# Sums of the last weights: in DRAM by copying and adding transfers during the SwiGLU pairs, in place of GpSimd sums inside the last product

## The chip, the cores and the metric

The kernel runs on one core of one Trainium2 chip. TensorE (PE) multiplies, PEld is its weight load, VectorE is DVE, ScalarE is ACT, GpSimd is POOL, and SyncE (SP) issues most DMA transfers. The metric is the device time of one execution in microseconds (us). The kernel before takes 820.69 us, the median of 3 runs (820.62 to 823.06).

## The reference, cut to what matters

One decoder block on 512 tokens of width 1024 in float32: a norm, one wide product `h @ w_in`, a causal convolution mixer and a recurrent mixer side by side, their merge through `w_mix_out`, then the SwiGLU channel mixer and a last norm. The change concerns the channel mixer:

```python
    h = rmsnorm(x, norm2_g[l])
    x = x + (jax.nn.silu(h @ ffn_w1[l]) * (h @ ffn_w3[l])) @ ffn_w2[l]
return rmsnorm(x, norm_f_g)
```

`ffn_w1` and `ffn_w3` are 1024 x 2816, `ffn_w2` is 2816 x 1024.

## The kernel before, in words

**Number format.** Every product in float32 is three products in fp32r: a tile is split into a rounded high part (ACT, line 120) and the rest (a subtraction, line 116, on DVE or POOL), and PE multiplies high by high, high by low and low by high. `wchunk` lists the weight pieces ("chunks", 128 x 1024 elements) in the order of use. `emit_chunk` loads one into a ring of `RAW` = 8 raw buffers (SP issues), and splits it into a ring of `HL` = 5 buffers (`hl_...`). `weights` emits `AHEAD` = 4 chunks ahead of the product that uses them.

**Seven products for eight.** The mixing product, the SwiGLU pairs and the last product multiply 2 x 2 blocks with seven block products, by the scheme of Winograd. From the four quarters b11, b12, b21, b22 of a weight piece it needs the sums t1, t2, t3 and t4, where t2 comes from t3, and t4 from t2. The left operands need such sums too; the results r1, r2, r5, r7 are added at the end.

**Stages in order of time.** (1) `w_in` with the convolutions beside it; (2) the two mixer outputs (`yb`, `ya`); (3) the mixing product (`mxr`); (4) the SwiGLU pairs, index k = 0 to 10, each seven products `fr` of 256-column halves, for `w1` and `w3` at once; (5) the last product `or` with `ffn_w2`, again 11 steps k, in three passes: a first (quarters b11, t1, b21), a second (b22, t2, t3) and a third (t4); (6) the final norm.

**SwiGLU weights.** Pairs 1 to 3 find their sums in DRAM (`fs`), made during stage 1. Pairs 4 to 10 go through `f_fly`: four quarters are loaded into raw buffers (`raw_fb`), and POOL makes the four sums in place, b12 and b11 in `sums_32`, b22 and b21 in `sums_14`. A sum overwrites its quarter, so it follows that quarter's own split on DVE.

**Weights of the last product.** `outq` is a `Quartered` with `fly=True`. Its method `fly` loads whole rows and quarters (lines 315, 324 and 341), and POOL makes the sums inside the raw buffers just before their split: t1 in the first pass (tile `raw_ob11`), t3, t2 and a copy of t2 in the second (`raw_ot2`, `ot2r`), t4 in the third (`raw_ot4`). DVE and ACT make the splits of all 40 chunks of this stage, and DVE also makes the sums and splits of the left operands (`ous`, `os1p`, `oe`, `ov`, then `oeb`, `ovb`).

**What sets the order.** Blocks under `manual_schedule` keep the named engines in the order of the program (stage 1, the end of the mixing product, the start of the pairs, the very end). Elsewhere, so in pairs and in most of the last product, the scheduler sets each engine's order, within `tc.issue_after`, which puts an instruction behind another one. Every engine then runs its own instructions strictly in order.

Of the kernel before, what the change touches and what calls it, by code (L numbers as in the profile page):

```python
# [8 lines left out]
F32 = mybir.dt.float32  # L9
# [4 lines left out]
P = 128  # L14
# [39 lines left out]
STORED = BEGUN + BEGUN_LATER  # L54
SUMS_AT, SUMS_STEP, SUMS_LAG, STORE_LAG = 3, 5, 2, 2
# [28 lines left out]
def tile_block(ctx, tc, a, out):  # L84
# [25 lines left out]


# [155 lines left out]
    class Quartered:  # L267
        def __init__(self, name, w, kh, lo, parts=(), step=None, on_pool=(), put_off=(), fly=False):
# [3 lines left out]
            self.step, self.lo = step or 1, lo  # L272
# [3 lines left out]
            self.all_sums = [] if fly else [dram.tile([P, 4, T], F32, tag=f"{name}t_{k}", name=f"{name}t_{k}") for k in range(kh)]  # L276
            self.sums = {(n, k): self.all_sums[k][:, i, :] for i, n in enumerate(IN_PLACE) if n not in parts and not fly for k in range(kh)}
# [18 lines left out]
            if fly:  # L296
                self.fly(chunk)
                return
# [7 lines left out]

        def fly(self, chunk):

            w, kh, lo, name = self.w, self.kh, self.lo, self.name
            b22, t2 = {}, {}  # L310

            def one(k):

                def load(raw_t):
                    nc.sync.dma_start(raw_t, w[:, self.tile(k, 0), :])
                    sub(pool_e, raw_t[:, T:], raw_t[:, T:], raw_t[:, :T])

                self.at["b11", k], self.at["t1", k] = ((f"{name}b11_{k}", i) for i in range(2))
                wchunk(f"{name}b11_{k}", load, 2, T, lo=lo)

            def two(k):

                def load(raw_t):
                    nc.sync.dma_start(raw_t, w[:, self.tile(k, 0), :])
                    r22, at = b22[k]
                    sub(pool_e, raw_t[:, T:], r22[:, at : at + T], raw_t[:, T:])
                    pool_e.tensor_tensor(out=raw_t[:, :T], in0=raw_t[:, T:], in1=raw_t[:, :T], op=ALU.add)
                    t2[k] = longt(f"{name}t2r{k}")
                    pool_e.tensor_copy(t2[k], raw_t[:, :T])

                self.at["t2", k], self.at["t3", k] = ((f"{name}t2_{k}", i) for i in range(2))
                wchunk(f"{name}t2_{k}", load, 2, T, lo=lo)

            def pair(n, k, then):
                of = [i for i in (k, k + 1) if i < kh]

                def load(raw_t):
                    for i, k_ in enumerate(of):
                        cs = slice(T * (int(n[2]) - 1), T * int(n[2]))
                        v = raw_t[:, i * T : (i + 1) * T]  # L340
                        nc.sync.dma_start(v, w[:, self.tile(k_, 1), cs])
                        then(k_, raw_t, i * T)

                for i, k_ in enumerate(of):
                    self.at["t4" if n == "b21" and then is four else n, k_] = (f"{name}{'t4' if then is four else n}_{k}", i)
                wchunk(f"{name}{'t4' if then is four else n}_{k}", load, len(of), T, lo=lo)

            def keep(k, raw_t, at):
                b22[k] = raw_t, at

            def four(k, raw_t, at):
                v = raw_t[:, at : at + T]
                sub(pool_e, v, v, t2[k])

            for k in range(kh):
                if k % 2 == 0:
                    pair("b21", k, lambda *a: None)
                one(k)
            for k in range(kh):
                if k % 2 == 0:  # L360
                    pair("b22", k, keep)
                two(k)
            for k in range(0, kh, 2):
                pair("b21", k, four)
# [20 lines left out]
        def make_sums(self, k):  # L385
# [4 lines left out]
            sub(vec, q22, q22, q12)  # L390
            sub(vec, q12, q12, q11)
            vec.tensor_tensor(out=q11, in0=q22, in1=q11, op=ALU.add)
            sub(vec, q21, q21, q11)
            if not self.parts:
                for i, v in enumerate(q):
                    nc.sync.dma_start(self.all_sums[k][:, 2 * i : 2 * i + 2, :], v.rearrange("p (m n) -> p m n", m=2))
                return
# [38 lines left out]
    def f_fly(k):  # L436
# [9 lines left out]

        def first():
            raw_t = new("b11")
            new("b12")
            return raw_t  # L450

        def sums_32():
            sub(pool_e, q["b12"], q["b22"], q["b12"])
            pool_e.tensor_tensor(out=q["b11"], in0=q["b12"], in1=q["b11"], op=ALU.add)  # L454

        def sums_14():
            sub(pool_e, q["b22"], q["b22"], q["b11"])
            sub(pool_e, q["b21"], q["b21"], q["b11"])
# [29 lines left out]
    def piece_sums(raw, dest, eng):  # L488
        if len(dest.shape) == 4:
            of = raw.rearrange("p (h k e n) -> p h e k n", h=2, k=2, e=2)  # L490
        else:
            of = raw.rearrange("p (h e n) -> p h e n", h=2, e=2)
# [6 lines left out]
    def piece_store(raw, dest, queue=nc.sync):  # L499
        if len(dest.shape) == 4:  # L500
            dest = dest.rearrange("p m k n -> p (m k) n")
# [1257 lines left out]
```

## Time and profile before

| | |
|---|---|
| median of 3 runs | 820.69 us |
| profiled execution | 821.84 us, of which the span (first to last instruction) is 820.1 us |
| PE busy | 788.0 us (96%), 4327 matmuls |
| DVE busy | 722.9 us (88%) |
| ACT busy | 470.9 us (57%) |
| POOL busy | 443.7 us (54%) |
| DMA moved | 135.57 MB, mean 165 GB/s |
| granted clock of TensorE, mean | 0.988 |

The span begins with the first instruction and ends with the last. A row of the timeline or the chain gives a start in us, a length in us, the engine and line, and the tile written and read. In a table by windows, each engine's busy time in that stretch stands with the number of its instructions, then the granted clock of TensorE (1.00 is full), the share of the time that the 16 DMA engines were busy, and GB/s. A group of instructions gives its count, busy time and the mean ns of one. Stage 4 lies from about 450 to 690 us, stage 5 from 675 to 814 us.

### The profile page before, as it was taken

The page shows a single profiled execution, that of the slowest core. Times are in us where ns is not written, and L with a number is a line of the kernel's source. Part 1 is how long each engine was busy: PE and PEld are TensorE (multiplying, and loading weights), DVE is VectorE, ACT ScalarE, POOL GpSimd, SP SyncE. Part 2 cuts the span into 40 slices and gives each one's busy share as a digit, 9 for nine tenths or more (in the row PEclk, how much of TensorE's full clock was granted, in tenths as well). Part 3 has the DMA queues.
Part 4 walks back from the last instruction along what each step waited for, and adds up shares of the span by engine and source line. Part 5 has one row for each costly group of instructions (what it writes and reads, how often), then busy time and mean ns, then how long its engine had stood idle before and what let it go on. Part 6 is the DMA issues. An engine that isn't in the chain of part 4 may idle for free.

```text
span 820.1 us, 12207 instructions
## 1 busy us (share of the span) xinstructions
PE 788.0 (96%) x4327; PEld 683.4 (83%) x4327; DVE 722.9 (88%) x959; ACT 470.9 (57%) x697; POOL 443.7 (54%) x265
## 2 busy tenths in 40 slices
PE   9999999999999999999999999999999999868776
PEld 8888888888888888888888989999999997656555
DVE  6489998998988977899978697799999999899997
ACT  7444769966775885572346765454544545535424
POOL 3366765765766446446103500366555644979970
PEclk9999999999999999999999999999999999988999
DMA  7827997986686335756675455433333344653312
GB/s 235 222 58 219 234 249 200 249 235 196 168 232 181 111 100 159 227 180 218 197 218 163 155 178 158 129 104 104 103 103 104 103 155 155 204 180 141 116 64 103
DMA packets 167951, 135.57 MB, mean 165 GB/s; under 512 B 12986, under 2 KB 143698, under 8 KB 167890
## 3 DMA queue, kind: packets, MB, share of 16 engines
q1 hardware_dynamic: 167154, 132.43, 54.9%
q0 software_dynamic: 576, 2.10, 0.7%
q8 instruction: 34, 0.56, 0.3%
q14 instruction: 27, 0.22, 0.1%
q10 hardware_dynamic: 160, 0.27, 0.1%
HBM read 109.07 MB, written 12.58 MB: 148 GB/s over the span
## 4 chain that ended last, share of the span: by engine, by line
PE 79%; DVE 12%; issue 3%; DMA 2%; POOL 2%; ACT 0%; SPq 0%; DVEq 0%; POOLq 0%; ACTq 0%
PE z L661 34%; PE fr L1480 18%; PE yb L661 7%; PE ya L661 5%; PE mxr L1287 5%; PE or L1287 4%; PE f L661 3%; POOL raw_ob L116 2%; PE g L1114 2%; DVE hl_ob L116 2%; DVE hl_ot L116 1%; DMA raw_ob<-in_ffn_w_dram 1%; DVE hl_ft L116 1%; PE fr L1534 1%; DVE hl_fb L116 1%
## 5 line engine op out<-in xcount | busy, mean ns | idle before, releaser
L116 POOL TENSOR_TENSOR hl_in<-raw_in,hl_in 128x1024 fp32r<-128x1024 f32 (+1 forms) x52 | 122.7, 2369 | 95.1 <-ACT hl_in L120 74.3
L914 DVE SCALAR_TENSOR_TENSOR cv<-u,par,cv 128x507 f32<-128x507 f32 (+15 forms) x240 | 162.2, 734 | 4.2 <-ACT cv L910 3.3
L116 POOL TENSOR_TENSOR raw_fb<-raw_fb,raw_fb 128x1024 f32<-128x1024 f32 x21 | 58.8, 2821 | 62.4 <-DMA raw_fb<-in_ffn_w_dram 51.0
L1480 PE MATMUL fr<-hs_0h,hl_ft 128*128 128x256 f32 x320 | 59.2, 283 | 0.0
L116 DVE TENSOR_TENSOR hl_fb<-raw_fb,hl_fb 128x1024 fp32r<-128x1024 f32 x29 | 50.6, 1747 | 5.6 <-ACT hl_fb L120 4.6
L120 ACT CAST hl_in<-raw_in 128x1024 fp32r<-128x1024 f32 x50 | 51.4, 1047 | 1.7 <-DMA th<-tg 0.8
L116 POOL TENSOR_TENSOR raw_ob<-raw_ob 128x512 f32<-128x512 f32 x11 | 35.6, 3248 | 28.7 <-DMA raw_ob<-in_ffn_w_dram 24.9
L1480 PEld LDWEIGHTS fr<-hs_0h,hl_ft 128*128 128x128 f32 x320 | 50.6, 192 | 0.0
L1480 PE MATMUL fr<-hs_0l,hl_ft 128*128 128x256 f32 x160 | 45.3, 283 | 0.0
L116 DVE TENSOR_TENSOR hl_ft<-raw_fb,hl_ft 128x1024 fp32r<-128x1024 f32 x28 | 44.3, 1580 | 0.4 <-ACT hl_ft L120 0.4
L116 POOL TENSOR_TENSOR hl_lo<-raw_lo,hl_lo 128x640 fp32r<-128x640 f32 x16 | 26.4, 1655 | 27.6 <-ACT hl_lo L120 27.6
L661 PE MATMUL z<-h10h,hl_in 128*128 128x512 f32 (+1 forms) x108 | 41.1, 382 | 0.0
L661 PE MATMUL z<-h12h,hl_in 128*128 128x512 f32 (+1 forms) x108 | 40.8, 379 | 0.0
L661 PE MATMUL z<-h15h,hl_in 128*128 128x512 f32 (+1 forms) x108 | 40.8, 379 | 0.0
L661 PE MATMUL z<-h14h,hl_in 128*128 128x512 f32 (+1 forms) x108 | 40.8, 379 | 0.0
L661 PE MATMUL z<-h16h,hl_in 128*128 128x512 f32 (+1 forms) x108 | 40.8, 379 | 0.0
L661 PE MATMUL z<-h13h,hl_in 128*128 128x512 f32 (+1 forms) x108 | 40.8, 379 | 0.0
L661 PE MATMUL z<-h11h,hl_in 128*128 128x512 f32 (+1 forms) x108 | 40.8, 379 | 0.0
L661 PE MATMUL z<-h17h,hl_in 128*128 128x512 f32 (+1 forms) x108 | 40.8, 379 | 0.0
L454 POOL TENSOR_TENSOR raw_fb<-raw_fb,raw_fb 128x1024 f32<-128x1024 f32 x7 | 18.8, 2688 | 37.9 <-issue 30.1
L120 ACT CAST hl_fb<-raw_fb 128x1024 fp32r<-128x1024 f32 x30 | 31.3, 1045 | 13.8 <-issue 5.4
L120 ACT CAST hl_ft<-raw_fb 128x1024 fp32r<-128x1024 f32 x28 | 28.6, 1046 | 17.5 <-POOL raw_fb L116 9.6
(948 smaller groups left out, 2761.9 us busy)
## 6 DMA issues: line engine op xcount, KB each, us to landing
raw_in<-in_w_in_dram SPq DMA_DIRECT2D x51, 512.0 KB
raw_fb<-in_ffn_w_dram SPq DMA_DIRECT2D x74, 256.0 KB
fws<-in_ffn_w_dram SPq DMA_DIRECT2D x12, 512.0 KB
raw_ob<-in_ffn_w_dram SPq DMA_DIRECT2D x22, 256.0 KB
raw_ob<-in_ffn_w_dram SPq DMA_DIRECT2D x11, 512.0 KB
raw_ot<-in_ffn_w_dram SPq DMA_DIRECT2D x11, 512.0 KB
raw_lo<-in_lru_w_out_dram SPq DMA_DIRECT2D x16, 320.0 KB
fs<-fws SPq DMA_DIRECT2D x8, 512.0 KB
```

The lines of the kernel that those rows point to most:

```text
L116: return eng.tensor_tensor(out=o, in0=x, in1=y, op=ALU.subtract)
L120: copy(h, full)
L454: pool_e.tensor_tensor(out=q["b11"], in0=q["b12"], in1=q["b11"], op=ALU.add)
L661: pe.matmul(ps, l, r, start=i == 0, stop=i == n - 1)
L914: vec.scalar_tensor_tensor(out=acc[:, s:], in0=u[c][:, : T - s], scalar=dw(c, s), in1=acc[:, s:], op0=ALU.mult, op1=ALU.add)
L1114: pe.matmul(ps[:HB], head_chunk[0][:ROWS_G, g, h % 2, m, :], ext[h][m][:ROWS_G], start=m == 0, stop=m == 1)
L1287: pe.matmul(banks[i][:, cs], l_[:, ts], r_[:, cs], start=start and n == 0, stop=stop and n == 2, skip_group_check=again)
L1480: pe.matmul(ps[:, HALVES[i]], lw[:, c, :], rx_, start=not (again or i or c or m), stop=bool(i and c == 3 and m == 2), skip_group_check=True,)
L1534: pe.matmul(self.r4[:, HALVES[i]], lw, rx_, start=not (i or c or m), stop=bool(i and c == 3 and m == 2), skip_group_check=True)
```

## The change

POOL no longer makes sums for `ffn_w2`. The sums stand in four DRAM tensors `ot1` to `ot4`, and transfers make them: `dram_sums` copies a quarter into place, and then adds another with a transfer that accumulates (`accum_op`). Since a transfer can add but not subtract, all sums have plus signs now, and the signs move to the left operands and to the sums of the results, instruction for instruction. `out_sums` makes 48 such transfers, 8 for each of six groups of two steps k (the last group has one), in the order all first jobs, all second jobs, and so on. POOL issues them in pairs 4 to 10 of stage 4, seven for each pair (the last call finds the list at its end): one after the second sum, three after the third, three after the fourth. `in_line` also fixes the order of the POOL sums of those pairs. In stage 5, SP loads the sums like any weight. One of the 40 splits, that of t4 for steps 6 and 7, is made by POOL rather than DVE.

```diff
-        def __init__(self, name, w, kh, lo, parts=(), step=None, on_pool=(), put_off=(), fly=False):
+        def __init__(self, name, w, kh, lo, parts=(), step=None, on_pool=(), put_off=()):
...
-            self.all_sums = [] if fly else [dram.tile([P, 4, T], F32, tag=f"{name}t_{k}", name=f"{name}t_{k}") for k in range(kh)]
-            self.sums = {(n, k): self.all_sums[k][:, i, :] for i, n in enumerate(IN_PLACE) if n not in parts and not fly for k in range(kh)}
+            self.all_sums = {n: dram.tile([P, kh, T], F32, tag=f"{name}{n}", name=f"{name}{n}") for n in IN_PLACE if n not in parts}
+            self.sums = {(n, k): v[:, k, :] for n, v in self.all_sums.items() for k in range(kh)}
...
-            if fly:
-                self.fly(chunk)
-                return
...
-        def fly(self, chunk):
...
-                    nc.sync.dma_start(raw_t, w[:, self.tile(k, 0), :])
-                    sub(pool_e, raw_t[:, T:], raw_t[:, T:], raw_t[:, :T])
...
-                    sub(pool_e, raw_t[:, T:], r22[:, at : at + T], raw_t[:, T:])
-                    pool_e.tensor_tensor(out=raw_t[:, :T], in0=raw_t[:, T:], in1=raw_t[:, :T], op=ALU.add)
-                    t2[k] = longt(f"{name}t2r{k}")
-                    pool_e.tensor_copy(t2[k], raw_t[:, :T])
...
-                sub(pool_e, v, v, t2[k])
...
+        def in_line(n, make, *what):
+            with tc.issue_after(newest["sum"]) if "sum" in newest else nullcontext():
+                newest["sum"] = make(pool_e, *what).ins
+            for _ in range(n):
+                next(out_steps, None)
...
         def sums_32():
-            sub(pool_e, q["b12"], q["b22"], q["b12"])
-            pool_e.tensor_tensor(out=q["b11"], in0=q["b12"], in1=q["b11"], op=ALU.add)
+            in_line(0, plus_on, q["b12"], q["b22"], q["b12"])
+            in_line(1, plus_on, q["b11"], q["b12"], q["b11"])
 
         def sums_14():
-            sub(pool_e, q["b22"], q["b22"], q["b11"])
-            sub(pool_e, q["b21"], q["b21"], q["b11"])
+            in_line(3, sub, q["b22"], q["b11"], q["b22"])
+            in_line(3, plus_on, q["b21"], q["b21"], q["b11"])
...
+    def dram_sums(quarter, sums):
+
+        b11, b12, b21, b22 = (quarter(i, h) for i in range(2) for h in range(2))
+        t1, t2, t3, t4 = (sums[n] for n in ("t1", "t2", "t3", "t4"))
+        copy = lambda o, x: pool_e.dma_start(o, x)
+        plus = lambda o, x: pool_e.dma_start(o, x, accum_op=ALU.add)
+        return [(copy, t1, b11), (plus, t1, b12), (copy, t3, b12), (plus, t3, b22), (copy, t2, t3), (plus, t2, b11), (copy, t4, t2), (plus, t4, b21)]
+
+    def out_sums():
+
+        rows = outq.w.rearrange("p (k i) n -> p i k n", i=2)
+        jobs = []
+        for k0 in range(0, KF, OUT_SUMS_OF):
+            ks = slice(k0, min(k0 + OUT_SUMS_OF, KF))
+            jobs.append(dram_sums(lambda i, h: rows[:, i, ks, h * T : (h + 1) * T], {n: v[:, ks, :] for n, v in outq.all_sums.items()}))
+        for start, dst, src in (one for of in zip(*jobs) for one in of):
+            with tc.issue_after(newest["sum"]):
+                start(dst, src)
+            yield
...
-    outq = Quartered("o", a["ffn_w2"][0].rearrange("(k p) n -> p k n", p=P), NF // 2, vec, step=2, fly=True)
+    outq = Quartered("o", a["ffn_w2"][0].rearrange("(k p) n -> p k n", p=P), NF // 2, vec, step=2, on_pool=("t4_6",))
...
+    out_steps = out_sums()
...
             s1 = shortt(f"{n}s1{k}")[:, LO]
-            add(s1, va[:, LO], va[:, HI])
+            sub(vec, s1, va[:, LO], va[:, HI])
...
-            sub(vec, e[:, LO], ua[:, HI], va[:, LO])
+            add(e[:, LO], ua[:, HI], va[:, LO])
...
+            less = lambda t, h, b_: sub(vec, sums[t][h], sums[t][h], b_)
...
-            plus(i, 1, r1[i])
-            plus(2 + i, 1, r1[i])
+            less(i, 1, r1[i])
+            less(2 + i, 1, r1[i])
             plus(i, 1, r2[i])
```

POOL in stage 4 before, between two pairs (8 and 9; `raw_fb12_8` is quarter b12 of pair 8):

```order
L454 TENSOR_TENSOR raw_fb11_8_6116<-raw_fb12_8_6119,raw_fb11_8_6116 128x1024
L116 TENSOR_TENSOR raw_fb12_9_6351<-raw_fb22_9_6420,raw_fb12_9_6351 128x1024
L116 TENSOR_TENSOR raw_fb21_8_6153<-raw_fb21_8_6153,raw_fb11_8_6116 128x1024
L116 TENSOR_TENSOR raw_fb22_8_6188<-raw_fb22_8_6188,raw_fb11_8_6116 128x1024
L454 TENSOR_TENSOR raw_fb11_9_6348<-raw_fb12_9_6351,raw_fb11_9_6348 128x1024
L116 TENSOR_TENSOR raw_fb12_10_6583<-raw_fb22_10_6665,raw_fb12_10_6583 128x1024
```

POOL at the same place now (`ot2` and `ot3` are the sums in DRAM, 128x2x512 is one quarter for two steps k):

```order
L114 TENSOR_TENSOR raw_fb12_8_6149<-raw_fb22_8_6218,raw_fb12_8_6149 128x1024
L114 TENSOR_TENSOR raw_fb11_8_6146<-raw_fb12_8_6149,raw_fb11_8_6146 128x1024
L486 DMA ot2_83<-ot3_86 128x1024
L120 TENSOR_TENSOR raw_fb22_8_6218<-raw_fb11_8_6146,raw_fb22_8_6218 128x1024
L486 DMA ot2_83<-ot3_86 128x512
L487 DMA ot2_83<-in_ffn_w2_dram 128x2x512 x2
L114 TENSOR_TENSOR raw_fb21_8_6183<-raw_fb21_8_6183,raw_fb11_8_6146 128x1024
L487 DMA ot2_83<-in_ffn_w2_dram 128x2x512 x3
L114 TENSOR_TENSOR raw_fb12_9_6388<-raw_fb22_9_6457,raw_fb12_9_6388 128x1024
```

The first sum of the next pair stood between the second and third sum of a pair, and t4's sum (`fb21`) ahead of t1's (`fb22`). Now the four sums of a pair stand together, t1's ahead of t4's, with seven transfers among and behind them.

POOL in stage 5 before, from the end of the first pass into the second:

```order
L116 TENSOR_TENSOR raw_ob11_9_7241<-raw_ob11_9_7241 128x512
L116 TENSOR_TENSOR raw_ob11_10_7316<-raw_ob11_10_7316 128x512
L116 TENSOR_TENSOR raw_ot2_0_7355<-raw_ob22_0_7322,raw_ot2_0_7355 128x512
L327 TENSOR_TENSOR raw_ot2_0_7355<-raw_ot2_0_7355 128x512
L116 TENSOR_TENSOR raw_ot2_1_7391<-raw_ob22_0_7322,raw_ot2_1_7391 128x512
L327 TENSOR_TENSOR raw_ot2_1_7391<-raw_ot2_1_7391 128x512
L116 TENSOR_TENSOR raw_ot2_2_7442<-raw_ob22_2_7400,raw_ot2_2_7442 128x512
L327 TENSOR_TENSOR raw_ot2_2_7442<-raw_ot2_2_7442 128x512
```

POOL there now, from its last sum of pair 10 to the end of the program:

```order
L114 TENSOR_TENSOR raw_fb21_10_6661<-raw_fb21_10_6661,raw_fb11_10_6624 128x1024
L487 DMA ot4_85<-in_ffn_w2_dram 128x2x512
L487 DMA ot4_85<-in_ffn_w2_dram 128x512
L120 TENSOR_TENSOR hl_ot4_6_7891<-raw_ot4_6_7888,hl_ot4_6_7891 128x1024
L1656 TENSOR_TENSOR of30_7945<-x2b30_7031,gfh_7033 128x256
```

Fifty-five instructions, 11 each of five kinds, have gone from stage 5; one split and the one product of the final norm that was there before are left. On PE the order of matmuls is unchanged; on DVE a few splits in the second pass have swapped places with a neighbour, and one has gone to POOL.

98 lines of the change are left out of this document (28 added, 70 removed).

## The prediction

> **What bounds the kernel now.** I read the busy time by windows first, to find where PE stops being full. All of it is one stretch of one view (columns: stretch and length, PE, PEld, DVE, ACT, POOL, granted clock, DMA share, GB/s).
>
> ```profile
> 640.00:680.00 40.00, 40.00 (x316) 39.18 (x316) 38.56 (x44) 21.28 (x33) 19.11 (x9) 1.00 0.45 146
> 680.00:700.00 20.00, 19.15 (x84) 15.21 (x83) 20.00 (x35) 11.51 (x18) 11.94 (x3) 1.00 0.52 171
> 700.00:720.00 20.00, 14.30 (x61) 10.94 (x59) 17.70 (x24) 11.37 (x19) 19.77 (x9) 0.98 0.51 171
> 720.00:740.00 20.00, 15.89 (x60) 12.28 (x61) 20.00 (x26) 6.82 (x8) 15.26 (x7) 0.85 0.64 210
> 740.00:760.00 20.00, 16.64 (x63) 13.22 (x62) 20.00 (x16) 9.88 (x16) 19.68 (x14) 0.83 0.36 127
> 760.00:780.00 20.00, 14.37 (x61) 10.92 (x59) 20.00 (x13) 9.79 (x13) 19.84 (x13) 1.00 0.32 110
> 780.00:800.00 20.00, 15.59 (x61) 12.27 (x61) 19.79 (x16) 5.50 (x9) 14.67 (x8) 0.91 0.19 66
> 800.00:821.00 21.00, 13.88 (x66) 11.34 (x65) 14.67 (x33) 8.24 (x21) 0.73 (x1) 0.93 0.27 101
> ```
>
> Up to 680 us PE is full at clock 1.00. In the last product it is not, while DVE and POOL are, and the clock falls. Next, the chain of waits, for what PE stands behind, and for the pace of the same kind of matmul where nothing holds it:
>
> ```profile
> 410.44 35.37 PE mxr L1287 x156
> ...
> 691.13 17.77 POOL raw_ob L116
> 708.93 1.06 ACT hl_ob L120
> 710.01 1.23 DVE hl_ob L116
> ...
> 798.23 14.16 PE or L1287 x60
> ...
> 813.91 0.43 DVE x2b L1236
> ```
>
> The mixing product has the same matmuls (128x512, line 1287): 35.37 / 156 = 0.227 us each. In the last product a POOL sum of 17.77 us stands on the path, then the split that waited for it. The instructions of tile `or` say how often (us, times):
>
> ```profile
>   DVE hl_ot L116: 28.3, 9
>   DVE hl_ob L116: 18.0, 8
> ```
>
> PE waits for DVE's splits (the view has PE and its weight load, and can count a wait twice). Why DVE is late, its groups by shape show, first from 684 to 708 us and then from 735 to 795 us:
>
> ```profile
> L116 DVE TENSOR_TENSOR hl_ob<-raw_ob,hl_ob 128x1024 fp32r<-128x1024 f32 x8 | 9.7, 1216 | 0.0
> ...
> L116 DVE TENSOR_TENSOR hl_ot<-raw_ot,hl_ot 128x1024 fp32r<-128x1024 f32 x11 | 23.5, 2144 | 0.2 <-ACT hl_ot L120 0.2
> ```
>
> The same split takes 1.216 us while POOL's sum is the one that crawls (those 17.77 us), and 2.144 us later, while POOL runs at its pace. Both read two tiles of SBUF, and one holds the other up. So the last product is bound by DVE and POOL together, not by PE.
>
> **The change part by part.**
>
> *Removed: POOL in the last product.* From 640 to 800 us:
>
> ```profile
> L116 POOL TENSOR_TENSOR raw_ob<-raw_ob 128x512 f32<-128x512 f32 x11 | 35.6, 3248 | 28.7 <-DMA raw_ob<-in_ffn_w_dram 24.9 <-DVE ov L1498 3.7
> L116 POOL TENSOR_TENSOR raw_ot<-raw_ob,raw_ot 128x512 f32<-128x512 f32 x11 | 24.7, 2248 | 4.6 <-DVE oe L116 4.6
> L116 POOL TENSOR_TENSOR raw_ot<-raw_ot,ot2r 128x512 f32<-128x512 f32 x11 | 21.4, 1972 | 0.0
> L327 POOL TENSOR_TENSOR raw_ot<-raw_ot 128x512 f32<-128x512 f32 x11 | 18.8, 1709 | 0.9
> L329 POOL COPY ot2r<-raw_ot 128x512 f32<-128x512 f32 x11 | 12.7, 1183 | 0.0
> ```
>
> These 113.2 us go. What PE then needs: its counts from 680 on are 456 matmuls, at 0.227 us 103.5 us, so they end at 783.5 instead of 813.9 us. That is 30.4 us: about 25 of idle time and 5 of low clock (the clock was 1.00 wherever PE was full). The 6.2 us behind 813.9 stay. Can DVE follow? From 690 to 800 us it runs
>
> ```profile
> 690.00:800.00 110.00, 85.93 (x341) 66.89 (x339) 107.49 (x108) 48.53 (x71) 98.10 (x47) 0.92 0.42 143
> ```
>
> 108 instructions, by shape 29 of 128x1024, 45 of 128x512, 33 of 128x256 and a small one. At the undisturbed 1.216, and by size 0.68 and 0.415, that is 80 us summed, and about 72 where each starts 0.075 us before the last one's end. PE's 341 matmuls take 77 us. So DVE keeps pace, with little to spare in the first pass (one and a half chunk splits, one of 512 and five of 256 columns, 4.0 us for a step, against 18 x 0.227 = 4.1 us) and more in the second, where the left operands' sums are done. I leave 3 us for the first step of each pass and for the one split that POOL now makes. Gain 27.4 us; without any spare on DVE half of it (rival one).
>
> *Added: POOL's issues in the pairs.* POOL, then ACT, at one pair; and the pair's 20 us:
>
> ```profile
> 607.46 2.48 POOL L454 TENSOR_TENSOR raw_fb<-raw_fb,raw_fb 128x1024 f32<-128x1024 f32 x1 [7.67 <-issue]
> 611.10 8.29 POOL L116 TENSOR_TENSOR raw_fb<-raw_fb,raw_fb 128x1024 f32<-128x1024 f32 x3 [1.16 <-DMA raw_fb<-in_ffn_w_dram]
> 627.07 2.40 POOL L454 TENSOR_TENSOR raw_fb<-raw_fb,raw_fb 128x1024 f32<-128x1024 f32 x1 [7.68 <-issue]
> ```
> ```profile
> 613.17 1.05 ACT L120 CAST hl_ft<-raw_fb 128x1024 fp32r<-128x1024 f32 x1
> ```
> ```profile
> 596.00:616.00 20.00, 20.00 (x169) 20.00 (x168) 19.46 (x17) 9.93 (x14) 11.17 (x5) 1.00 0.37 107
> ```
>
> A pair lasts about 20 us (627.07 - 607.46 = 19.6 here), POOL is busy 11 of it, and about 9 are free for seven issues, 1.3 us each. The second sum ends at 609.9, but the split of t2 begins on ACT only at 613.17: 3 us of cover. Now t1's sum comes earlier than before, t4's about as early, behind four issues. The trace has four issues by POOL of 128 rows of 4 KB:
>
> ```profile
> L502 POOL DMA_DIRECT2D fs<-fws x4: 769/770/917, 241.0 to 321.6; - x4
> ```
>
> Low bound 7 x 0.77 = 5.4 us: hidden. An issue with 256 rows and an accumulation isn't in the trace; twice the row, 1.54 us, makes 10.8 us, so a pair of 21.8 us, 1.7 us late for each of seven. I take 1 us (the rows are more, not the bytes): hidden. Range 0 to 12 us. Nothing excludes a small gain here: POOL's first two `raw_ob` sums, in the pairs, go too.
>
> *Added: the transfers themselves.* A copy moves 11 x 256 KB x 4 = 11.53 MB, the accumulations as much. What a byte costs the engines, from the DMA view of 690 to 790 us (rows of 2 and 4 KB, packets, MB, share of 16 engines), and what is free from the first sums of pair 4 to those of pair 10:
>
> ```profile
> q1 hardware_dynamic: 6685, 15.65, 46.3%
> ```
> ```profile
> 532.00:668.00 136.00, 136.00 (x1135) 136.00 (x1135) 130.59 (x115) 67.69 (x98) 77.41 (x29) 1.00 0.34 102
> ```
>
> 0.463 x 16 x 100 / 15.65 = 47.3 engine-us per MB. Copies cost 545 engine-us, 34 us of all 16. Accumulations are not in the trace: at least the same (34 us), and if target and source are both read one after the other, twice (68 us). Free are 0.66 x 136 = 90 us. At once the cost all is hidden; at twice, 102 us are 12 more than free. Each transfer depends on the one six before it, so POOL runs up to six ahead, 6/7 of a pair or 17 us, which covers the 12, though not every load then comes in time. I take twice, the nearest description of what such a transfer does, with 3 us of delay in all; low bound 0, high bound three times: 136 us, 46 late, less 17 is 29 us. If they did not share the 16 engines with the loads, the term would be 0, its low bound.
>
> *Moved signs and loads.* Additions and subtractions swap one for one on DVE, in the same shapes, so 0. SP loads the 40 chunks in 256 KB pieces: the same bytes in 22 issues more, on a queue that mostly waits; I put them at 0.4 us in all. The DMA share above (0.19 to 0.64) leaves room for them in a last product of 105 us: 15.65 MB in 100 us becomes about 19 MB, a share near 0.6.
>
> *Sum.* 30.4 - 3 - 3.4 (transfers 3, and 0.4 for SP's added issues) = 24 us. The profiled execution has 821.84 us, 1.74 more than its span and 1.15 more than the median: 821.84 - 24 = 797.8 profiled, and 820.69 - 24 = 796.7, so **797 us** as median.
>
> **The rivals.**
>
> *One: the five split buffers take the place of POOL.* ACT may fill a buffer only when PE has left it.
>
> ```profile
>   ACT hl_ot L120: 12.6, 8
> ```
>
> ACT waited for PE 12.6 us in eight times in that tile's rows. If PE, ACT and DVE go in turns there, half the 30.4 us stay idle: 820.7 - 15.2 + 3.4 = 809 us. Against it: the mixing product ran with the same buffers without a gap. Chance 0.20.
>
> *Two, slower: accumulating transfers starve POOL's queue.* POOL waits in order, so a transfer that isn't done holds the sums of the pair, then ACT, DVE and PE. At three times the cost of a copy 29 us are lost against 27.4: it decides from there. At four times: 34 + 136 = 170 us, 80 late, less 17 is 63 us, thus 856 us; between them I name 830 us. For it: nobody here has measured one; against it: 90 us free. The Trainium skill ("DMA: Bandwidth & Descriptors", Specifications) puts a core's HBM limit at about 358 GB/s; estimate: copies at two times and accumulations at three times 11.53 MB, with 102 GB/s of loads, are 71.5 MB, so 200 us for 136, 47 late after the 17, and 840 us. No run here shows it: the fastest of the page's 40 slices has 249 GB/s.
>
> ```profile
> GB/s 235 222 58 219 234 249 200 249 235 196 168 232 181 111 100 159 227 180 218 197 218 163 155 178 158 129 104 104 103 103 104 103 155 155 204 180 141 116 64 103
> ```
>
> This rival's chance is 0.13.
>
> *Three, slower: the issues are held off by DVE.* DVE is busy 19.46 of 20 us there, and POOL's sum of 17.77 us shows what a busy DVE can do to it. From 1.9 us for an issue on (0.6 over the 1.3 us that are free, 49 times) all gain is gone; at 2.1 us it is 832 us. Against it: most of the four issues of 0.77 us lie in a stretch with DVE at 91.52 of 100 us.
>
> ```profile
> 200.00:300.00 100.00, 100.00 (x442) 82.11 (x441) 91.52 (x133) 74.29 (x94) 60.23 (x40) 1.00 0.60 170
> ```
>
> By the Trainium skill ("SBUF — State Buffer", Who interferes with whom) two-input DVE instructions take the shared read interface, and descriptor writing needs the write one, which it marks as inferred; by it an issue would stay near 0.77 us. The trace agrees as far as those four go. This rival's chance is 0.07.
>
> *Four: no effect.* The loads of sums in stage 5 wait for transfers that end late, and PE idles as before: 820 us. Against it: all of t2's are issued by the start of pair 9 and t4's with pair 10, before the passes that use them begin. Chance 0.05.
>
> **How the numbers follow.** My forecast, 788 to 805 us, has 0.55; the rivals 0.20, 0.13, 0.07 and 0.05. The likeliest is 797 us. Forecast, rival one and four together, 785 to 820 us, are 0.80. What this measurement can tell from no change is 0.3%, 2.5 us. Faster: 0.55 + 0.20 = 0.75. Slower: 0.20. Same: 0.05.
>
> **What would show it.** In the profile after: POOL nearly empty from 690 us on; `hl_ot` at 1.2 us, not 2.1; matmuls `or` at 0.227 us and the clock at 1.00; rows of POOL's issues near 1 us and a DMA share in the pairs of 0.8 or more with PE at 20.00 of 20. Wrong would be PE below 20.00 before 680 us with POOL waiting for transfers (rivals two, three), or PE waiting on ACT, and ACT on PE, in the last product (rival one).

## The result and the profile after

| | median us | lowest to highest | runs |
|---|---|---|---|
| before | 821.45 | 820.62 to 823.06 | 4 |
| after | 811.08 | 811.05 to 812.55 | 4 |

The ratio is 0.9876, with a 95% interval of 0.9855 to 0.9897. The change makes the kernel 10.4 us faster. The forecast was 24 us, so the direction is right and the size is not.

To see where the missing part went, I split the time at the start of the last product. The rows of tile `or` give the first and last start of each group of its matmuls; the group with `ous0h` is the first one of the product. Before, then after:

```profile
L1287 PE MATMUL or<-hl_ob,ous0h x8: 389/391/397, 675.2 to 677.5; 128*128 128x512 f32 x8
```
```profile
L1247 PE MATMUL or<-hl_ob,ous0h x8: 389/391/397, 697.9 to 700.2; 128*128 128x512 f32 x8
```

The last product begins 22.7 us later than before (697.9 - 675.2). From there to the end of the span it was 820.1 - 675.2 = 144.9 us and is 809.3 - 697.9 = 111.4 us, so it gained 33.5 us. The sum, 10.8 us, is the difference of the two spans. The last product did what was forecast and 6 us more; the SwiGLU pairs before it lost what was thought to be free.

Busy time by windows, after (stretch and length, PE, PEld, DVE, ACT, POOL, granted clock, DMA share, GB/s):

```profile
540.00:560.00 20.00, 20.00 (x169) 20.00 (x168) 19.97 (x17) 8.51 (x12) 12.66 (x9) 1.00 0.96 207
560.00:580.00 20.00, 16.67 (x117) 16.47 (x116) 19.96 (x15) 7.88 (x11) 11.39 (x9) 0.83 1.09 272
...
660.00:680.00 20.00, 16.07 (x115) 15.86 (x114) 20.00 (x19) 8.73 (x13) 10.09 (x8) 0.83 0.76 220
...
700.00:740.00 40.00, 40.00 (x178) 33.15 (x177) 39.97 (x75) 26.48 (x41) 0.00 (x0) 1.00 0.78 259
```

From 700 us on PE is full at clock 1.00 and POOL is empty, as forecast. In the pairs PE falls to 16 of 20 us and the clock to 0.83 with it. DVE is busy all the time there. POOL is not: it stands empty for 7 to 10 of 20 us in these windows. The DMA share is near 1. The chain of waits, after, through one pair and at the end:

```profile
573.50 4.60 DMA raw_fb<-in_ffn_w_dram
...
583.02 5.15 DVE ov L1459
...
698.09 103.39 PE or L1247 x456
```

The chain names two suspects. One is a load of a pair's weights that takes 4.6 us. The other is the multiply at line 1459 that writes half of `ov` from `q`. DVE's groups by shape from 550 to 650 us, before and then after, say what that multiply used to take:

```profile
L1498 DVE TENSOR_TENSOR ov<-q 128x256 f32<-128x256 f32 x5 | 4.3, 854 | 0.0
```
```profile
L1459 DVE TENSOR_TENSOR ov<-q 128x256 f32<-128x256 f32 x4 | 23.7, 5932 | 0.0
```

Its mean was 0.85 us and is 5.9, and DVE counts as busy all that time. What POOL does meanwhile, and then DVE, in the timeline of one pair after (start, length, engine; POOL's TENSOR_TENSOR rows are the sums of t1 and of t4 and the first sum of the next pair):

```profile
579.48 2.46 POOL L120 TENSOR_TENSOR raw_fb<-raw_fb,raw_fb 128x1024 f32<-128x1024 f32 x1 [3.04 <-DVE hl_fb L120]
581.88 1.92 POOL L486 DMA_DIRECT2D ot<-in_ffn_w_dram  x3
583.81 2.41 POOL L114 TENSOR_TENSOR raw_fb<-raw_fb,raw_fb 128x1024 f32<-128x1024 f32 x1
586.15 3.54 POOL L487 DMA_DIRECT2D ot<-in_ffn_w_dram  x3
588.32 3.81 POOL L114 TENSOR_TENSOR raw_fb<-raw_fb,raw_fb 128x1024 f32<-128x1024 f32 x1
```
```profile
580.18 2.83 DVE L120 TENSOR_TENSOR hl_ft<-raw_fb,hl_ft 128x1024 fp32r<-128x1024 f32 x1
582.94 5.22 DVE L1459 TENSOR_TENSOR ov<-q 128x256 f32<-128x256 f32 x1
588.09 0.68 DVE L113 TENSOR_TENSOR c<-fr,c 128x512 f32<-128x512 f32 x1
588.69 4.53 DVE L120 TENSOR_TENSOR hl_ft<-raw_fb,hl_ft 128x1024 fp32r<-128x1024 f32 x1
```

The sum of t1 ends at 581.9, three copies are issued, the sum of t4 runs, three adding transfers are issued, and the first sum of the next pair follows. DVE's multiply stands from 582.94 until 588.2, and the split after it until the next sum has ended. The addition that reads a product in PSUM (`c<-fr,c`, 0.68 us) is not held.

### The profile page after: what moved, and what is told of

It reads as the page before. It is cut to its first block, busy times and chain, and to the rows that moved or that the text cites. A ratio compares the mean times of both kernels' runs of the same rounds, so it can differ in the third digit from the quotient of the medians.

```text
span 809.3 us, 12207 instructions
## 1 busy us (share of the span) xinstructions
PE 787.3 (97%) x4327; PEld 687.8 (85%) x4327; DVE 712.1 (88%) x958; ACT 471.5 (58%) x697; POOL 366.3 (45%) x259
## 4 chain that ended last, share of the span: by engine, by line
PE 78%; DVE 15%; DMA 3%; issue 2%; SPq 0%; POOL 0%; ACT 0%; DVEq 0%; ACTq 0%
PE z L621 35%; PE or L1247 13%; PE fr L1441 7%; PE yb L621 7%; PE ya L621 5%; PE mxr L1247 5%; DVE ov L1459 5%; DVE hl_ft L120 4%; PE f L621 3%; DVE hl_fb L120 2%; PE g L1074 2%; DMA raw_fb<-in_ffn_w_dram 2%; DVE c L113 1%; PE fr L1495 1%; DVE q L120 1%
## 5 line engine op out<-in xcount | busy, mean ns | idle before, releaser
L114 POOL TENSOR_TENSOR raw_fb<-raw_fb,raw_fb 128x1024 f32<-128x1024 f32 x21 | 63.5, 3026 | 86.9 <-DMA raw_fb<-in_ffn_w_dram 45.5
L1441 PE MATMUL fr<-hs_0h,hl_ft 128*128 128x256 f32 x320 | 66.3, 304 | 13.6 <-DVE hl_ft L120 13.6
L1441 PEld LDWEIGHTS fr<-hs_0h,hl_ft 128*128 128x128 f32 x320 | 55.7, 211 | 14.8 <-DVE hl_ft L120 14.8
L1458 ACT ACTIVATE c<-c 128x256 f32<-128x256 f32 x30 | 12.2, 416 | 74.6 <-DVE c L113 74.6
L120 DVE TENSOR_TENSOR hl_ft<-raw_fb,hl_ft 128x1024 fp32r<-128x1024 f32 x28 | 52.8, 1887 | 0.0
L1441 PE MATMUL fr<-hs_0l,hl_ft 128*128 128x256 f32 x160 | 48.0, 300 | 0.0
L120 POOL TENSOR_TENSOR hl_ot<-raw_ot,hl_ot 128x1024 fp32r<-128x1024 f32 x1 | 2.4, 2400 | 100.6 <-ACT hl_ot L124 100.6
L114 POOL TENSOR_TENSOR fws<-fws 128x256 f32<-128x256 f32 x48 | 36.5, 761 | 2.7
```

Source lines behind the costliest of these rows:

```text
L114: plus_on = lambda eng, o, x, y: eng.tensor_tensor(out=o, in0=x, in1=y, op=ALU.add)
L120: return eng.tensor_tensor(out=o, in0=x, in1=y, op=ALU.subtract)
L1441: pe.matmul(ps[:, HALVES[i]], lw[:, c, :], rx_, start=not (again or i or c or m), stop=bool(i and c == 3 and m == 2), skip_group_check=True,)
L1458: act.activation(c[:, LO], c[:, LO], AF.Silu)
```

## The experiments

Three theories fit the trace after. **Order:** the four sums of a pair now stand in line, one behind the other, and that alone holds DVE. **Traffic:** the transfers take the DMA engines when a pair's loads are due (the 4.6 us). **Issue:** the instructions by which GpSimd starts the transfers, between its sums, hold DVE. Ratios below are against the kernel before on the same chip, with 95% intervals.

**e1: no transfers.** The order of the sums stays.

```diff
-                if n[0] == "t":
+                if n[0] == "t" and name != "o":
                     return self.sums[n, k]
+                if n[0] == "t":
+                    n = "b" + {"1": "11", "2": "12", "3": "22", "4": "21"}[n[1]]
...
-    out_steps = out_sums()
+    out_steps = iter(())
```

> Left out: the 48 transfers; the last product loads the plain weights where it loaded the sums, as many bytes from as many rows, so the numbers it computes are others. GpSimd's four sums of each pair keep their new order. Theory order (the four sums standing together behind one another hold VectorE): the pairs keep their 24 us, 806 to 811 us. Theories issue and traffic (below) both: the pairs go back to 20 us each, so 811 less 7 pairs of 2.5 to 2.8 us, 790 to 794 us.

787.94 us (787.70 and 788.17), ratio 0.9589 (0.9561 to 0.9618). The theory of order is out: the four sums in line cost nothing. The transfers, one way or another, cost 811.1 - 787.9 = 23 us, all of what the pairs lost. (This run and the next lie 2 us below the 790 us that were expected at the least with the pairs free.) The multiply of `ov` from 550 to 650 us in e1, for later:

```profile
L1461 DVE TENSOR_TENSOR ov<-q 128x256 f32<-128x256 f32 x5 | 13.1, 2620 | 0.0
```

The sums in line, without any issue, do hold it, for 2.6 us against 0.85 before, but PE stays full.

**e2: the same traffic, not issued by GpSimd.** The loads of the last product are those of e1.

```diff
-        copy = lambda o, x: pool_e.dma_start(o, x)
-        plus = lambda o, x: pool_e.dma_start(o, x, accum_op=ALU.add)
+        copy = plus = lambda o, x: nc.sync.dma_start(o, x)
...
-            with tc.issue_after(newest["sum"]):
+            with tc.issue_after(newest["any"]):
                 start(dst, src)
```

> The 48 transfers are plain copies (nothing is added) and SyncE issues them, seven behind the loads of each pair; the last product loads plain weights where it loaded the sums. GpSimd issues none. Theory issue: 790 to 796 us, since GpSimd is as free as without transfers. Theory traffic: most of the 18 us stay lost, 803 to 811 us, less what copies move less than additions. Theory order: 806 to 811 us.

787.88 us (787.87 and 787.89), ratio 0.9589 (0.9561 to 0.9616): as without transfers. The windows and then the chain of waits of e2:

```profile
540.00:560.00 20.00, 20.00 (x169) 20.00 (x169) 19.75 (x18) 9.20 (x14) 10.09 (x5) 1.00 0.97 301
```
```profile
499.89 175.08 PE fr L1442 x1459
674.97 103.39 PE or L1248 x456
```

With a DMA share of 0.97 and 301 GB/s, more than the 207 of the changed kernel in the same window, PE stays full, and the whole chain from 500 us on is PE. The traffic of the copies costs nothing, and the loads of 4.6 us that stood in the changed kernel's chain were no cause: with more bytes per second, e2 has no load in its chain. (In the window from 560 us its DMA share is 0.84 against 1.09, so what additions load the engines with beyond copies is left to the next run.)

**e4: the same issues, an eighth of the bytes.** The loads of the last product are those of e1.

```diff
-                start(dst, src)
+                start(dst[:, :, :64], src[:, :, :64])
```

> Left out: seven eighths of each transfer's columns (64 of 512 are moved, in as many rows), and the last product loads plain weights where it loaded the sums. GpSimd issues the same 48 transfers at the same places. Theory issue (the 0.5 to 1.6 us that each issue takes on GpSimd, between its sums, hold VectorE's additions on the same memory port): as the changed kernel, 806 to 811 us. Theory traffic (the transfers take the DMA engines when the pair's own loads are due): 790 to 796 us. Theory order: 806 to 811 us.

810.70 us (810.52 and 810.87), ratio 0.9866 (0.9837 to 0.9895): the changed kernel's time, without its bytes. Busy time by windows, and DVE's group from 550 to 650 us:

```profile
560.00:580.00 20.00, 16.69 (x127) 16.49 (x126) 19.97 (x15) 7.96 (x11) 11.39 (x9) 0.91 0.50 124
```
```profile
L1461 DVE TENSOR_TENSOR ov<-q 128x256 f32<-128x256 f32 x4 | 20.9, 5223 | 0.0
```

The DMA share is 0.50 where the changed kernel has 1.09, PE is down to 16.69 all the same, and the multiply is held 5.2 us. Together with e2 this is the answer to traffic or issue: it is the issues.

**e3: no additions.** All 48 transfers are copies, issued by GpSimd at the same places.

```diff
-        plus = lambda o, x: pool_e.dma_start(o, x, accum_op=ALU.add)
+        plus = copy
```

> The 24 adding transfers are plain copies too, issued by GpSimd at the same places, so the sums hold the last quarter copied and the output is another. Theory issue: an adding transfer took 1.58 us to issue on GpSimd and a copy 0.52 to 0.70, so 24 us of GpSimd's 53 go and about half of the loss with them, 798 to 803 us. Theory traffic: it depends on what an addition moves more than a copy; if its engine time is twice a copy's, a third of the 105 us goes, 800 to 806 us; if the same, 809 to 811.

803.50 us (803.33 and 803.66), ratio 0.9779 (0.9750 to 0.9807). The instructions on tile `ot` show the issues, min/median/max in ns, after and in e3:

```profile
L487 POOL DMA_DIRECT2D ot<-in_ffn_w_dram x24: 825/1576/3034, 539.9 to 684.4; - x24
L486 POOL DMA_DIRECT2D ot<-in_ffn_w_dram x12: 547/695/2374, 528.5 to 583.2; - x12
L486 POOL DMA_DIRECT2D ot<-ot x12: 515/541/1275, 607.5 to 660.4; - x12
```
```profile
L488 POOL DMA_DIRECT2D ot<-in_ffn_w_dram x36: 544/696/730, 528.4 to 678.0; - x36
```

An adding issue is recorded with 1.58 us, but the records of three in a row overlap (3.54 us for three above, so 1.18 each); a copy's issue takes 0.5 to 0.7 us. Half a microsecond less on each of 24 issues saved 7.6 us in all, and 15.6 us stay lost with the shorter ones.

**e7: an eighth of the rows.** The loads of the last product are those of e1.

```diff
-                start(dst, src)
+                start(dst[:16], src[:16])
```

> Left out: seven eighths of each transfer's rows (16 partitions of 128 are moved, in their full width), and the last product loads plain weights where it loaded the sums. GpSimd issues the same 48 transfers at the same places. If an issue's time goes by the rows it describes, it falls from 0.5 to 1.6 us to some 0.2 and the pairs go back to 20 us: 789 to 796 us. If an issue costs a fixed time: as the run with few columns, 808 to 811 us.

808.24 us (808.22 and 808.27), ratio 0.9830 (0.9810 to 0.9849). The same view, e7:

```profile
L489 POOL DMA_DIRECT2D ot<-in_ffn_w_dram x24: 768/1043/1997, 539.4 to 680.5; - x24
L488 POOL DMA_DIRECT2D ot<-in_ffn_w_dram x12: 508/518/1658, 528.7 to 581.4; - x12
```

Neither form of the expectation held fully, but it is near the fixed time: an eighth of the rows took 0.69 us to 0.52 and 1.58 to 1.04, and 20 of the 23 us stayed lost. Making the transfers smaller is no way out. Their place is, as the next run shows; fewer of them in the same places were not tried.

**e5: another place.** All seven issues of a pair stand behind its first sum. The second sum has to wait for DVE there anyway.

```diff
-            in_line(0, plus_on, q["b12"], q["b22"], q["b12"])
-            in_line(1, plus_on, q["b11"], q["b12"], q["b11"])
+            in_line(7, plus_on, q["b12"], q["b22"], q["b12"])
+            in_line(0, plus_on, q["b11"], q["b12"], q["b11"])
...
-            in_line(3, sub, q["b22"], q["b11"], q["b22"])
-            in_line(3, plus_on, q["b21"], q["b21"], q["b11"])
+            in_line(0, sub, q["b22"], q["b11"], q["b22"])
+            in_line(0, plus_on, q["b21"], q["b21"], q["b11"])
```

> Nothing left out: each pair's seven issues stand in one row behind the first of its four sums, ahead of the 5.6 us in which GpSimd stands empty before the second; none stands between the other sums. Theory port (an issue holds VectorE's two-operand instructions wherever it runs): the 4.6 to 6 us of issues hold the splits that VectorE runs there, 803 to 813 us. Theory gap (the issues cost time only because they stand between the sums and so leave VectorE no gap to get in): 790 to 797 us.

796.36 us (794.55 and 798.15), ratio 0.9685 (0.9656 to 0.9714): 15 of the 23 us come back, with every transfer kept. POOL and then DVE in the timeline of one pair of e5:

```profile
584.92 3.16 POOL L487 DMA_DIRECT2D ot<-in_ffn_w_dram  x3
586.89 2.76 POOL L486 DMA_DIRECT2D ot<-ot  x3
591.48 0.52 POOL L486 DMA_DIRECT2D ot<-ot  x1 [1.83 <-DMA ot<-in_ffn_w_dram]
```
```profile
585.98 0.41 DVE L1459 TENSOR_TENSOR ov<-c 128x256 f32<-128x256 f32 x1
586.32 1.21 DVE L120 TENSOR_TENSOR hl_ft<-raw_fb,hl_ft 128x1024 fp32r<-128x1024 f32 x1
```

While GpSimd issues from 584.92 to 589.65, DVE's multiply takes its 0.41 us and the split behind it 1.21. So an issue by itself holds nothing, which ends the plain form of the theory (an issue holds DVE wherever it runs). Some of the 8 us that remain over e1 are seen in the third row: the last issue of the row waits 1.83 us for an earlier transfer, and the second sum, which stands behind it, is late. More is seen in e5's chain of waits:

```profile
544.92 18.58 DMA raw_fb<-in_ffn_w_dram
...
593.40 13.12 DMA raw_fb<-in_ffn_w_dram
```

Two loads of a pair's weights take 18.6 and 13.1 us here, where the longest such load in the chain after takes 4.6. The DMA share stands between 0.99 and 1.11 in the four windows from 540 to 620 us. So seven transfers started in a row look as if they held up loads: traffic, which did not matter at the places of the change, seems to matter here. What each of the two parts costs was not measured apart.

**e8: other work in the same places.** GpSimd fills a dead tile in the place of each issue. The loads of the last product are those of e1.

```diff
-        copy = lambda o, x: pool_e.dma_start(o, x)
-        plus = lambda o, x: pool_e.dma_start(o, x, accum_op=ALU.add)
+        copy = lambda o, x: [pool_e.memset(par[:, :n], 0.0) for n in (400, 200)][-1]
+        plus = lambda o, x: [pool_e.memset(par[:, :400], 0.0) for _ in range(3)][-1]
...
-                start(dst, src)
+                newest["sum"] = start(dst, src).ins
```

> Left out: the transfers; the last product loads plain weights where it loaded the sums. In the place of each of the 48 issues GpSimd fills a dead tile of constants with zeros, about as long as an issue (two fills, some 0.7 us, for a copy; three, some 1.2 us, for an adding transfer). Theory gap (any work of GpSimd between two of its sums costs as much, because VectorE, held behind one sum, meets the next one): 803 to 812 us, with the multiply that writes ov held 5 us again. Theory issue proper (the writing of descriptors holds VectorE, fills don't): 788 to 794 us, ov at 2.6 us.

791.09 us (790.91 and 791.28), ratio 0.9628 (0.9610 to 0.9645). POOL and then DVE in one pair of e8:

```profile
574.24 2.53 POOL L120 TENSOR_TENSOR raw_fb<-raw_fb,raw_fb 128x1024 f32<-128x1024 f32 x1 [2.93 <-DVE hl_fb L120]
576.72 2.37 POOL L488 MEMSET par<- 128x400 f32 x6
579.05 3.13 POOL L114 TENSOR_TENSOR raw_fb<-raw_fb,raw_fb 128x1024 f32<-128x1024 f32 x1
```
```profile
577.77 0.41 DVE L1461 TENSOR_TENSOR ov<-q 128x256 f32<-128x256 f32 x1
...
578.71 1.21 DVE L120 TENSOR_TENSOR hl_ft<-raw_fb,hl_ft 128x1024 fp32r<-128x1024 f32 x1
```

The fills take longer than the issues (2.37 us against 1.92 between these two sums), and the multiply comes at the same point, 1.0 us after the end of t1's sum. Yet it takes 0.41 us (2.6 were expected), and the loss is 3 us, not 23. Lateness of the sums is not the cause.

So DVE's two-input instructions were met in four surroundings. Issues with a sum behind them that follows at once (the changed kernel): held 5.2 us. Issues with no sum ready behind them (e5): not held. Fills with a sum behind them that follows at once (e8): not held. Sums in line with nothing between them (e1): held 2.6 us, about one sum. By these four, what holds DVE for so long is the two together: GpSimd's issues, and a sum standing ready behind them. The row of the sum at 588.32 above fits this: it is recorded from 588.32 on with 3.81 us, 1.4 more than a sum's 2.41, since the issues before it end only at 586.15 + 3.54 = 589.69, and DVE's split that began at 588.69 is held already then. Since GpSimd's records overlap in this way, the trace does not say whether the sum took hold early or ran later than its record.

By the Trainium skill ("SBUF — State Buffer", Who interferes with whom) a two-input DVE instruction contends with a GpSimd instruction that reads SBUF and not with one that only writes, and it infers that the writing of descriptors needs the write interface. The 0.41 us beside the fills and the 1.21 us beside the issues of e5 agree with that. The same page of the Trainium skill (SBUF: two separate sides) says that whichever of the two starts first has the port pair for its whole instruction; the 5.22 us, which begin before t4's sum and end 1.9 us after it, are not told by that, and the measurement decides.

**e10 and e11: one half each.** Four issues stand behind the first sum, and three between t1's and t4's (e10) or between t4's and the next pair's first (e11).

```diff
-            in_line(0, plus_on, q["b12"], q["b22"], q["b12"])
-            in_line(1, plus_on, q["b11"], q["b12"], q["b11"])
+            in_line(4, plus_on, q["b12"], q["b22"], q["b12"])
+            in_line(0, plus_on, q["b11"], q["b12"], q["b11"])
...
-            in_line(3, plus_on, q["b21"], q["b21"], q["b11"])
+            in_line(0, plus_on, q["b21"], q["b21"], q["b11"])
```

In e11 the last two lines are the other way round: none behind t1's sum, three behind t4's.

> Nothing left out: of each pair's seven issues four stand behind the first sum (a sum that waits for VectorE comes next) and three between t1's sum and t4's, which is ready by then. Theory ready sum (issues of GpSimd cost VectorE time where a sum that is ready stands behind them; behind the first sum, where the next one isn't ready, they cost little: 794.6 and 798.2 us with all seven there): 800 to 805 us, ov held about 5 us. Theory amount (it is the number of issues in the pair, wherever they stand): as with all seven behind the first sum, 794 to 798 us.

> As the run before, but the three stand between t4's sum and the next pair's first sum, which is ready by then too. Theory ready sum: 800 to 805 us again; the two together make up the changed kernel's 811, so 16 us over the two above some 795. Theory amount: 794 to 798 us.

e10: 802.36 us (801.58 to 803.28, 4 runs), ratio 0.9769 (0.9752 to 0.9785). e11: 798.15 us (797.03 to 799.77, 4 runs), ratio 0.9717 (0.9703 to 0.9732). POOL and DVE in one pair of e10, then DVE's group of e11 from 550 to 650 us and a split of its timeline:

```profile
578.22 3.51 POOL L487 DMA_DIRECT2D ot<-in_ffn_w_dram  x3
580.38 6.11 POOL L114 TENSOR_TENSOR raw_fb<-raw_fb,raw_fb 128x1024 f32<-128x1024 f32 x2
```
```profile
579.27 7.50 DVE L1459 TENSOR_TENSOR ov<-q 128x256 f32<-128x256 f32 x1
```
```profile
L1459 DVE TENSOR_TENSOR ov<-q 128x256 f32<-128x256 f32 x5 | 13.1, 2622 | 0.0
```
```profile
582.22 6.13 DVE L120 TENSOR_TENSOR hl_ft<-raw_fb,hl_ft 128x1024 fp32r<-128x1024 f32 x1
```

In e10 the multiply that begins during the three issues waits through both sums behind them, 7.5 us. In e11, with no issue between t1's and t4's sums, it takes 2.62, the same as in the run without transfers. There the split beside the other three issues is held instead, until 1.1 us after the sum behind them has ended: 6.1 us in two of these five pairs, where e1 has 2.8. So the hold moves with the issues. e10's time came out as the theory of the ready sum said; e11's did not, it lies at the edge of the other one. Three issues cost 6 us over e5 in the first place. In the second they cost 1.8, which is not clear of the spread of e5's own two runs. Together that is 7.8 us, where the changed kernel has 14.7 over e5. The two places don't add up; what the rest is was not taken apart, and e11's chain, like e5's, has a late load in it (10.5 us).

**e6: all transfers early.** Copies by SyncE in the last 24 steps of the first stage, each t then a single adding transfer: t1 = b11 + b12, t3 = b12 + b22, t2 = b11 + t3, t4 = b21 + t2. GpSimd issues 12 of them from about 390 us and 12 from about 470 us, where it is empty.

```diff
+            copies.append([(t1, b11), (t3, b12), (t2, b11), (t4, b21)])
+            sums.append([(t1, b12), (t3, b22), (t2, t3), (t4, t2)])
...
+        for dst, src in out_copy:
+            nc.sync.dma_start(dst, src)
+            yield
...
+            if at >= len(ORDER) - 24:
+                next(out_steps, None)
...
+    out_adds(12, [newest["sub"]])
...
+    out_adds(12, fulls[-8:])
```

> The same sums, by 24 copies that SyncE issues in the last 24 steps of the first stage (about 200 to 390 us) and 24 adding transfers that GpSimd issues in its two empty stretches (12 from about 390 us, 12 from about 470 us); none in the pairs. Theories port and gap both free the pairs: 788 to 791 us if VectorE has room in those stretches (15 to 17 of 20 us busy). By theory port VectorE's splits (1.22 us each) are seen held to 2 us and more while the issues run, with up to 4 us of loss, 788 to 795 us; by theory gap they keep 1.22 us there, since no sum of GpSimd's is near. If GpSimd's issues wait for the copies or for one another, the first sums of pair 4 come late and 795 to 805 us.

791.41 us (790.51 to 795.17, 4 runs), ratio 0.9640 (0.9614 to 0.9666). The windows of e6, and a row of DVE's timeline:

```profile
420.00:440.00 20.00, 19.55 (x87) 15.86 (x86) 12.50 (x18) 8.51 (x11) 0.00 (x0) 1.00 1.08 275
440.00:460.00 20.00, 19.28 (x124) 16.85 (x123) 17.13 (x38) 12.98 (x33) 8.00 (x9) 1.00 0.99 290
...
580.00:600.00 20.00, 20.00 (x169) 20.00 (x168) 19.45 (x17) 10.13 (x14) 10.75 (x5) 1.00 0.37 106
```
```profile
424.03 0.69 DVE L113 TENSOR_TENSOR x<-mxr,x 128x512 f32<-128x512 f32 x1 [4.71 <-DMA x<-in_x_dram]
```

The pairs are free again, PE at 20.00. Beside nine adding issues in a row (390.9 to 401.3 us), with no sum behind them, DVE's splits take 1.22 us: as in e5, issues alone hold nothing. What is left looks like a matter of traffic: DVE waits 4.7 us for loads of x beside the first twelve adding transfers, and PE loses 0.45 and 0.72 us in two windows. The rest of the 3.5 us over e1 was not traced.

**e9: the better place for half of them.** As e6, but t1's and t3's additions come from 470 us on, and t2's and t4's two by two behind the first sum of pairs 4 to 9.

```diff
-    out_adds(12, [newest["sub"]])
...
             in_line(plus_on, q["b12"], q["b22"], q["b12"])
+            out_adds(min(2, len(out_add)), [newest["sum"]])
```

> Nothing left out. 24 copies by SyncE in the last 24 steps of the first stage; the 12 adding transfers of t1 and t3 by GpSimd in its empty stretch from 470 us, those of t2 and t4 two by two behind the first sum of a pair (pairs 4 to 9), ahead of its empty 5.6 us; none from 390 us, where the run with all transfers early had PE wait for the loads of x. Theories gap and issue: each pair of issues (2.3 us) fits in the 5.6 us, the pairs stay at 20 us, 787 to 791 us. If behind the first sum issues still cost what they did there (796 with seven per pair, 8 above no issues; so two cost 2 to 3), 790 to 793 us.

789.51 us (788.78 to 790.50, 5 runs), ratio 0.9612 (0.9599 to 0.9625), with all sums computed: 32 us faster than before, where the change as made has 10.4, and 1.6 us from the run without transfers. Its windows in the pairs:

```profile
580.00:600.00 20.00, 20.00 (x169) 20.00 (x168) 19.97 (x17) 10.05 (x14) 12.35 (x7) 1.00 0.68 158
```

## Why the prediction was right and wrong

*What bounds the kernel, and "Removed: POOL in the last product": right, a little small.* The pace was right: the chain has 456 matmuls in 103.39 us, 0.227 us each. `or` waits no more, POOL is empty there, the clock is 1.00. That the count agrees with the forecast's 456 is luck. Those were to be the matmuls from 680 us on, and the trace before has 448 of them there; the chain's 456 are the whole product but its last 12. 448 at 0.227 us are 101.7 us, so the term is 813.9 - 680 - 101.7 = 32.2 us before anything is set aside, where the prediction has 30.4. The 3 us set aside for the first steps of the passes made it 27.4, and they were not needed, since PE is full from the first matmul to the last; measured are 33.5. Rival one, the five split buffers, fell with that. That its 809 us lie beside the measured 811 is luck: the time was lost in the pairs, not in the last product.

*"Added: POOL's issues in the pairs": this step failed.* It took 1 us for an issue, "hidden" in 9 free microseconds of POOL, at most 12 us of loss. The price of an issue was near enough (0.5 to 1.2 us) and POOL does have the time: it is empty for 7 to 10 of 20 us in the windows after. The step asked only whether POOL's time suffices. The loss is on DVE, which the prediction had itself at 19.46 of 20 us, and 22.7 us stand where it had 0. e4 shows that they come from the issues, e8 and e5 that it takes issues with a sum ready behind them.

The "3 us of cover" for t2's split speak of the same oversight: they look at when a sum is done, and not at how long DVE is held meanwhile.

*"Added: the transfers themselves": the size was right, the delay was not there.* The page's rows of GpSimd's queue (packets, MB, share of 16 engines), after, in e3 and in e1 without transfers:

```profile
q0 software_dynamic: 9792, 25.17, 13.6%
```
```profile
q0 software_dynamic: 6976, 25.17, 9.5%
```
```profile
q0 software_dynamic: 576, 2.10, 0.8%
```

With the spans of 809.3, 801.5 and 786.4 us that is 110.1, 76.1 and 6.3 us of all 16 engines. 48 copies cost 69.8, so 24 cost 34.9 (forecast 34), and 24 additions 110.1 - 6.3 - 34.9 = 68.9 us (forecast at twice a copy, 68). But of the 3 us of delay taken for it nothing is seen: e2 has the traffic of 48 copies beside the pairs and no loss. That the additions' further 34 us cost nothing either was shown only with few bytes (e4) and not apart, and only at the places of the change: with the transfers in a row, e5 has loads of 13 and 19 us in its chain.

*Rival two, starved by slow transfers, fell* with the same rows: the price is twice, not three times, and POOL waits for DVE, not for transfers. *Rival three* had the right place and the two engines the wrong way round: not DVE holds the issues off, the issues, with the sum behind them, hold DVE off. Its threshold, 1.9 us for an issue, is not reached in the median (1.58 at most, and 1.18 without the overlap), and its end, all gain gone, did not come.

*The sum.* Forecast -27.4 + 0 + 3 + 0.4 = -24; measured -33.5 + 22.7 = -10.8 us in the spans. Had the pairs stayed free, as they are in e2, the time would have been 787.9, and the forecast 9 us too slow.

*The signs to look for.* All of them for the last product came (`hl_ot` at 1.22 us in the mean), and so did the DMA share of 0.8 and more in the pairs, but without PE at 20.00. "PE below 20.00 before 680 us" came too, though not "with POOL waiting for transfers".

## What to carry to other kernels

Before work is put on an engine "because it has the time", look at which other engine its instructions hold up: the price is paid on that one, and busy time does not show it, since an instruction that is held counts as busy (an `ov` of 0.41 us read as 5.9). GpSimd's DMA issues are cheap where no sum of its own stands ready behind them, so put them in front of one of its waits (two in a row in e9, which is 1.6 us above the run without transfers; seven in a row in e5 are 8 us above it) or into a stretch where it is empty, and give plain copies to SyncE, which cost nothing here at a DMA share of 0.97. When a chain of waits names both a load and a held instruction, take them apart with two runs, the traffic without the issues and the issues without the traffic, before either is mended.

## What the runs showed of the hardware that was not expected

- Issues of GpSimd with a ready sum of GpSimd behind them hold a two-input DVE instruction from before the sum until up to 1.9 us after it (5.2 us for a product of 0.41; 7.5 us where a second sum follows). Neither alone does it: issues without a ready sum hold nothing (e5, e6), and sums without issues hold the same product for 2.6 us (e1). By what mechanism DVE is let in late, after the sum has ended by its record, stays open.
- An adding DRAM-to-DRAM transfer costs the DMA engines twice a copy (68.9 us for 24, against 34.9), and GpSimd 1.2 us to issue against 0.5 to 0.7. An eighth of the rows takes a quarter to a third off the issue (1.58 to 1.04 us, 0.69 to 0.52), an eighth of the bytes nothing (1.56 us).
- Much of what looks like a full DVE in the pairs is waiting for GpSimd's four sums. DVE's splits from 550 to 650 us in e1, without transfers, and a window of e8:

```profile
L120 DVE TENSOR_TENSOR hl_ft<-raw_fb,hl_ft 128x1024 fp32r<-128x1024 f32 x20 | 40.4, 2020 | 0.0
```
```profile
560.00:580.00 20.00, 20.00 (x169) 20.00 (x169) 16.64 (x16) 9.88 (x14) 16.30 (x20) 1.00 0.37 104
```

The splits take 2.02 us in the mean there and 1.21 when nothing holds them, and e8 has PE at 20.00 beside a DVE at 16.64. An engine at 19.46 of 20 can have room left, and the held time is where to look for it.
